# A hybrid attention and SSD layer: head-pair scores in three groups of six banks, and ScalarE emptying every product bank

## The chip, the cores and the metric

The kernel runs on one core of a Trainium2 chip. The time is the device time of one execution in microseconds, and what counts is the median of the runs. One execution was also profiled; the numbers of the trace come from that one.

## What is computed

One decoder layer on a sequence of 1024 tokens, 1024 wide, in float32. A modulated RMS norm feeds one input projection, whose columns are queries, keys, values and a gate of 16 attention heads (64 wide) and the inputs of a Mamba-2 SSD mixer with its own gate. Cut to what matters here:

```python
proj = h @ w_in                     # 1024 x 6672
# attention, per head, swept over 128-query blocks:
z = einsum("bqhd,bkhd->bhqk", q[:, start:end], k[:, :end]) * 64**-0.5
log_one_minus = where(mask, log_sigmoid(-z), 0.0)
tail = cumsum(log_one_minus, axis=3, reverse=True) - log_one_minus
weights = exp(where(mask, log_sigmoid(z) + tail, -inf))
o = einsum("bhqk,bkhd->bqhd", weights, v[:, :end])
y_attn = rms_norm(o, sb_norm_gain) * silu(z_attn)
# SSD: conv, softplus(dt), chunked scan in 128-token chunks
y_ssm = rms_norm(y * silu(z_ssm), ssm_norm_gain)
x = x + gate * (concat([y_attn, y_ssm]) @ w_out)
return rms_norm(x, norm_f_gain)
```

## The kernel before

Float32 products are made of three matmuls: an operand is split into a rounded high part and the rest (`whi`, `wlo`; `hh`, `hl`), and high times high, high times low and low times high are added up in one bank of PSUM. A product of 128 features by 1024 tokens (`inproj_f`) goes in two halves of 512 columns, each 24 matmuls into one bank of the pool `pj`.

The program has a first part (norm, modulation, convolution inputs), a middle one (the SSD scan), and from about 311 us on the attention of eight head pairs. From there the order of instructions on each engine is the order in which the code is written (`K` and `pinned`). The attention needs little of TensorE at a time and waits on ScalarE and VectorE, so it is laced into the remaining matrix products, called the side work (`inproj_f`, `inproj_v`, `outproj`): `ROUND` lists the steps of one pair, and after each of them `fill` runs side steps. `left` says how many microseconds of the current bank's product are still to come, `tick` advances a planned clock, and on it `late` emits ScalarE's and VectorE's share of the attention little by little.

The steps of a pair, both heads (`e` = 0, 1) together:
- `scores` ("s"): the products of queries and keys. Each head uses 64 rows of TensorE's array, so the two heads run side by side (mode 64 x 128). `GROUPS` says which query blocks `i` and which columns stand in which bank. A group takes four banks of the pool `pz`, and there are five groups per pair.
- `sigmoids` on ScalarE from each bank into `om` (or `bc`) and `be` (or `bs`), then `scan` and `weights` on VectorE, which leave the weights in `be` / `bs`.
- `turned` ("t"): 128 x 128 transposes of the weights on TensorE, two banks at a visit, copied back by ScalarE. One bank is of the pool `pt`, the second of `pj`, the pool of the side products.
- `values` ("v"): weights times values, each head in 64 columns of the array (mode 128 x 64), in the bank `pv`.

PSUM has eight banks: `pj` 2, `pz` 4, `pt` 1, `pv` 1. A side product's bank is emptied in different ways: queries and keys by ScalarE twice (`qk`); the two gates by a ScalarE function and then by a VectorE instruction that reads the bank again (`zgate_evac`, `gate_ssm`, L959 and L848); the SSD output projection by VectorE alone (`out_ssm`, L1227). `by_v` and `slow` mark such products. `turn` is the last gate's product, laced with loading and splitting `w_out`; `front` and `back` do that for the attention half.

Of the kernel before, what the change touches and what calls it, by code (L numbers as in the profile page):

```python
# [14 lines left out]
P = 128  # L15
# [11 lines left out]
def hybrid_layer_kernel(  # L27
# [68 lines left out]


# [88 lines left out]
    left, slow = [0.0], [False]  # L186
# [111 lines left out]
    def inproj_f(col, evac, between=None, by_v=False):  # L298


        wts = take(2) if pinned[0] else split_f(load_f(col))
        for b in range(2):
            ps = bank(pj, "pj")
            for k in range(KT):
                mm_f(ps, wts, k, b)
                if pinned[0]:
                    ahead()
                    if b and k % 4 == 3:
                        used()
                left[0], slow[0] = 0.7 * (KT - 1 - k), by_v  # L310
                yield 0.7
            evac(b, ps)
            if between:
                yield between(b)

    def inproj_v(vc, with_dt, v_tiles, dt_raw, extra=None):
# [19 lines left out]
        for i in range(TB):  # L336
            ps = bank(pj, "pj")
            ts_ = slice(i * P, (i + 1) * P)
            for k in range(KT):
# [500 lines left out]
    def gate_ssm(j):  # L840
        box = []

        def evac(b, ps):
            if b == 0:
                box.append(mk(sp, "th", [P, S], bufs=1))
            th, sl = box[0], slice(b * HALF, (b + 1) * HALF)
            A.activation(th[:, sl], ps, AF.Tanh, scale=0.5)
            V.scalar_tensor_tensor(th[:, sl], th[:, sl], 1.0, ps, op0=ALU.add, op1=ALU.mult)  # L848
            V.tensor_tensor(xs[j][:, sl], xs[j][:, sl], th[:, sl], op=ALU.mult)

        yield from inproj_f(C_ZS + j * P, evac, by_v=True)
# [77 lines left out]
    def qk(p, box):  # L929
# [3 lines left out]
        def evac(b, ps):  # L933
# [19 lines left out]
    def zgate_evac(p):  # L953
        def evac(b, ps):
# [4 lines left out]
            V.scalar_tensor_tensor(zg, zg, cols[:, 92 + p:93 + p], ps, op0=ALU.mult, op1=ALU.mult)  # L959
# [3 lines left out]
    def zgate(p):  # L963
        yield from inproj_f(C_Z + p * P, zgate_evac(p), by_v=True)
# [3 lines left out]
    GROUPS = {7: ((7, 0, 512, 0, 0), (7, 512, 512, 1, 0)), 6: ((6, 0, 512, 0, 0), (6, 512, 384, 1, 0)),  # L968
# [3 lines left out]


    ROUND = (("s", 7, 0), ("t", 3, -1), ("t", 2, -1), ("v", 2, -1), ("v", 0, -1), ("s", 6, 0), ("t", 7, 0),
             ("s", 5, 0), ("t", 6, 0), ("s", 4, 0), ("t", 5, 0), ("t", 1, 0), ("s", 3, 0), ("t", 4, 0),
             ("t", 0, 0), ("f", 0, 0), ("v", 6, 0), ("v", 4, 0))
# [9 lines left out]
    def scores(p, g):  # L986
        qh, ql, kh, kl = box[p]
        flush("A", lambda: not late["A"])
        n_ = seq["made"]
        flush("V", lambda: len(seq["scanned"]) >= n_ - 1)  # L990
        seq["made"] += 1
        if g % 2:
            tiles[p, g // 2] = [duo() if g > 3 else mk(sp, "bs", [P, 2, HALF], bufs=2) for _ in range(2)]
        oms = [mk(op, "om", [P, 1028], bufs=2), mk(sp, "bc", [P, S], bufs=4)]
        parts = []
        zs = [[bank(pz, "pz") for _ in range(2)] for _ in range(2)]
        for i, c0, cw_, b, z0 in GROUPS[g]:
            mw = max(cw_, 256)

            for n, (a, k_) in enumerate(((qh, kh), (qh, kl), (ql, kh))):  # L1000
                for e in range(2):
                    r = slice(64 * e, 64 * e + 64)
                    K(T.matmul(zs[b][e][:, z0:z0 + mw], a[r, i * P:(i + 1) * P], k_[r, c0:c0 + mw],  # L1003
                               start=(n == 0), stop=(n == 2)))
            parts.append((i, c0, cw_, [z[:, z0:z0 + cw_] for z in zs[b]]))
        off = {i: 0 if i == g else (g + 1) * P for i, _, _, _ in parts}

        def sigmoids(i, c0, cw_, z, e):
# [3 lines left out]
            be, om = tl[e][:, i % 2, x0:x0 + W], oms[e][:, off[i] + c0:off[i] + c0 + cw_]  # L1012
# [6 lines left out]
        def scan(i, e):  # L1019
            W = (i + 1) * P  # L1020
            om = oms[e][:, off[i]:off[i] + W]

            diag, rest = om[:, W - P:W][:, ::-1], om[:, 0:W - P][:, ::-1]
            V.tensor_tensor_scan(diag, diag, ident[:, ::-1], 0.0, op0=ALU.mult, op1=ALU.max)
            if i:
                V.tensor_tensor_scan(rest, rest, rest, om[:, W - P:W - P + 1],
                                     op0=ALU.mult, op1=ALU.bypass)

        def weights(i, e):
            W = (i + 1) * P  # L1030
            tl, x0 = place(p, i)
            be, om = tl[e][:, i % 2, x0:x0 + W], oms[e][:, off[i]:off[i] + W]
            V.memset(be[:, W - 1:W], 0.0)
            V.tensor_tensor(be[:, :W - 1], be[:, :W - 1], om[:, 1:W], op=ALU.mult)
            seq["weights"].add((p, i, e))
            if e == 1 and i == parts[-1][0]:
                seq["scanned"].append((p, g))

        for e in range(2):
            for i, c0, cw_, zs in parts:  # L1040
                cost = 0.3 + 1.6e-3 * cw_
                late["A"].append((cost, lambda i=i, c0=c0, cw_=cw_, z=zs[e], e=e: sigmoids(i, c0, cw_, z, e)))
        tick(1.8)

    def turned(p, i):

        banks = [(e, j0, min(i + 1, j0 + 4)) for e in range(2) for j0 in range(0, i + 1, 4)]

        while banks:
            wide = sum(b[2] - b[1] for b in banks[:2]) > 4  # L1050
            while wide and side_left() and left[0] >= 0.0 and not 1.3 < left[0] < (2.2 if slow[0] else 3.6):
                side_step()
            n = 1 if wide and left[0] < 0.0 else 2
            go, banks = banks[:n], banks[n:]
            for e, _, _ in go:
                if (p, i, e) not in seq["weights"]:
                    flush("A", lambda: (p, i, e) in seq["weights"] or not late["A"])
                    flush("V", lambda: (p, i, e) in seq["weights"])
            room, used_, copies = bank(pt, "pt"), 0, []
            for e, j0, j1 in go:  # L1060
                tl, x0 = place(p, i)
                be = tl[e][:, i % 2, x0:x0 + (i + 1) * P]
                if used_ + j1 - j0 > 4:
                    room, used_ = bank(pj, "pj"), 0
                for j in range(j0, j1):
                    K(T.transpose(room[:, (used_ + j - j0) * P:(used_ + j - j0 + 1) * P],  # L1066
                                  be[:, j * P:(j + 1) * P], ident))
                copies.append((be[:, j0 * P:j1 * P], room[:, used_ * P:(used_ + j1 - j0) * P]))
                used_ += j1 - j0
            for to, from_ in copies:  # L1070
                A.copy(to, from_)
            tick(0.11 * sum(j1 - j0 for _, j0, j1 in go))
            fill(sum(0.5 + 0.1 * (j1 - j0) for _, j0, j1 in go), True)

    def values(p, i0):
        (tl, x0), hb, q0 = place(p, i0), i0 // 4, i0 % 4
        if i0 in (6, 2):
            while side_left() and clock[0] < free_at[0]:
                side_step()
            pav[p] = bank(pv, "pv")  # L1080
        for j in range(i0 + 2):
            u = int(j > i0)
            for e in range(2):
                K(T.matmul(pav[p][64 * e:64 * e + 64, (q0 + u) * P:(q0 + 2) * P],  # L1084
                           vs[p][:, j * P + 64 * e:j * P + 64 * e + 64],
                           tl[e][:, u:2, x0 + j * P:x0 + (j + 1) * P], start=(j == 0), stop=(j > i0)))
        tick(0.2 * i0 + 0.4)
        if i0 in (6, 2):
            return
        sl = slice(hb * HALF, (hb + 1) * HALF)  # L1090
        if p == 0 and hb == 1:
# [12 lines left out]
        if hb == 0:
# [10 lines left out]
    def outproj(w_h, w_l, evac, first=None):  # L1115

        yt = take(2)
        for b in range(2):
            ps = first if first is not None and b == 0 else bank(pj, "pj")
            sl = slice(b * HALF, (b + 1) * HALF)  # L1120
            for k in range(KT):
# [7 lines left out]
                left[0], slow[0] = 0.7 * (KT - 1 - k), True  # L1129
# [11 lines left out]
    def turn():  # L1141
# [49 lines left out]
        for k, b in [(k, b) for k in range(6) for b in range(2)] + [(6, 0), (7, 0), (6, 1), (7, 1)]:  # L1191
# [21 lines left out]
    def out_ssm():  # L1213
# [6 lines left out]
        for i in range(TB):  # L1220
            t3 = []

            def evac(sl, ps):
                hooks["first"] = True
# [5 lines left out]
            yield from outproj(lambda k, b: wo_h[k][:, b * HALF:(b + 1) * HALF],  # L1230
                               lambda k, b: wo_l[k // 2, b][:, k % 2], evac, None if i else bank(pz, "pz"))
# [83 lines left out]
    def count(what, i):  # L1315
        if what == "s":
            return 4.0
        if what in "vf":
            return 0.0
        return 2 * sum(0.5 + 0.1 * (min(i + 1, j0 + 4) - j0) for j0 in range(0, i + 1, 4))  # L1320
# [47 lines left out]
    for p in range(9):  # L1368
        for what, i, before in ROUND:
# [142 lines left out]
```

## Time and profile before

| | |
|---|---|
| median of 3 runs | 1063.65 us (1063.28 to 1064.63) |
| the profiled execution: its time, its span | 1063.0 us, 1061.3 us |
| granted TensorE clock | 0.999 of full speed |
| TensorE matmul busy | 1039.0 us, 98% of the span |
| VectorE busy | 768.0 us, 72% |
| ScalarE busy | 528.6 us, 50% |
| the eight pairs, 311 to 925 us: TensorE, VectorE, ScalarE busy | 605.2, 456.0, 322.1 us of 614 |

A time is 1.7 us over the span in the profiled execution; the median is 0.65 us over that execution. A matmul's shown duration reaches past the start of the next one, because matmuls overlap in the array: what one costs is read from one start to the next.

### The profile page before, as it was taken

How to read it: one execution, taken by the hardware profiler on the slowest of the kernel's cores; microseconds unless marked ns; L12 is line 12 of the kernel's file. 1: busy time of each engine (PE TensorE's matmuls, PEld its weight loads, DVE VectorE, ACT ScalarE, POOL GpSimd, SP SyncE). 2: the span in 40 equal slices, each digit the busy share in tenths (PEclk: the TensorE clock that was granted, in tenths of full speed). 3: DMA queues.
4: the chain of work that ended last, by engine and by line, in shares of the span. 5: the costliest groups of instructions: out<-in, count | busy, mean ns of one | idle time of the engine just before them, and what ended most of it. 6: DMA issues, size and time to landing. Idle time of an engine off the chain costs nothing.

```text
span 1061.3 us, 16252 instructions
## 1 busy us (share of the span) xinstructions
PE 1039.0 (98%) x6317; PEld 844.2 (80%) x6317; DVE 768.0 (72%) x1339; ACT 528.6 (50%) x1162; POOL 2.6 (0%) x23
## 2 busy tenths in 40 slices
PE   7999999999999999999999999999999999999997
PEld 5789888777877787798787987878977777688886
DVE  5728779988848775656787758877668789665554
ACT  5755397676423553563554644646546646410111
POOL 0000000000000000000000000000000000000000
PEclk9999999999999999999999999999999999999999
DMA  9611332223202221101321103211111632665432
GB/s 350 229 41 31 92 112 79 74 95 129 71 20 70 80 70 31 60 21 41 91 59 61 31 21 90 76 35 41 39 52 30 199 97 74 204 210 174 155 110 79
DMA packets 91560, 96.15 MB, mean 91 GB/s; under 512 B 5998, under 2 KB 75994, under 8 KB 91484
## 3 DMA queue, kind: packets, MB, share of 16 engines
q1 hardware_dynamic: 88828, 86.45, 25.9%
q10 hardware_dynamic: 2656, 8.67, 2.4%
q8 instruction: 49, 0.80, 0.3%
q14 instruction: 27, 0.22, 0.1%
HBM read 78.26 MB, written 16.84 MB: 90 GB/s over the span
## 4 chain that ended last, share of the span: by engine, by line
PE 86%; DVE 8%; ACT 2%; issue 2%; DMA 1%; ACTq 0%; DVEq 0%; SPq 0%
PE pj L295 35%; PE pj L1125 13%; PE pv L1084 6%; PE pz L1003 5%; PE pz L553 3%; PE pt L1066 3%; PE pj L345 3%; PE pj L341 3%; PE pj L342 3%; DVE om L62 2%; PE pj L1066 2%; DVE bc L62 2%; PE pz L815 1%; PE pv L829 1%; PE pz L820 1%
## 5 line engine op out<-in xcount | busy, mean ns | idle before, releaser
L295 PE MATMUL pj<-hh,whi 128*128 128x512 f32 x544 | 222.2, 408 | 0.0
L295 PE MATMUL pj<-hh,wlo 128*128 128x512 f32 x544 | 214.1, 394 | 0.0
L295 PE MATMUL pj<-hl,whi 128*128 128x512 f32 x544 | 212.5, 391 | 0.0
L295 PEld LDWEIGHTS pj<-hh,whi 128*128 128x128 f32 x544 | 102.3, 188 | 24.5 <-issue 5.6
L295 PEld LDWEIGHTS pj<-hh,wlo 128*128 128x128 f32 x544 | 102.1, 188 | 22.7 <-issue 0.7
L295 PEld LDWEIGHTS pj<-hl,whi 128*128 128x128 f32 x544 | 102.5, 188 | 19.1 <-issue 1.0
L62 DVE TENSOR_TENSOR wlo<-raw,whi 128x512 fp32r<-128x512 f32 (+1 forms) x109 | 75.4, 692 | 23.1 <-ACT whi L62 16.7
L62 ACT COPY be<-pt 128x512 f32<-128x512 f32 (+2 forms) x98 | 47.1, 499 | 82.7 <-PE pt L1066 79.7
L62 ACT ACTIVATE be<-pz 128x255 f32<-128x255 f32 (+5 forms) x160 | 84.6, 531 | 0.0
L62 DVE TENSOR_TENSOR_SCAN om<-om 128x896 f32<-128x896 f32 (+6 forms) x56 | 71.9, 1285 | 2.0
L62 DVE TENSOR_TENSOR_SCAN bc<-bc 128x896 f32<-128x896 f32 (+6 forms) x56 | 71.9, 1285 | 2.0
L62 DVE TENSOR_TENSOR_SCAN om<-om,ident 128x128 f32<-128x128 f32 x64 | 26.9, 421 | 62.3 <-ACT om L62 62.2
L62 ACT ACTIVATE om<-pz 128x512 f32<-128x512 f32 (+1 forms) x96 | 48.0, 500 | 36.1 <-PE pz L1003 36.1
L341 PE MATMUL pj<-whi,hh 128*128 128x256 f32 (+1 forms) x224 | 65.1, 291 | 0.0
L1003 PE MATMUL pz<-big,big 64*128 64x512 f32 (+2 forms) x576 | 63.5, 354 | 1.1 <-ACT be L62 0.9
L345 PE MATMUL pj<-whi,hl 128*128 128x256 f32 (+1 forms) x224 | 64.4, 288 | 0.0
L342 PE MATMUL pj<-wlo,hh 128*128 128x256 f32 (+1 forms) x224 | 63.6, 284 | 0.0
L62 ACT ACTIVATE th<-v 128x1024 f32<-128x1024 f32 (+2 forms) x9 | 8.5, 943 | 103.7 <-DVE v L62 103.7
L1003 PEld LDWEIGHTS pz<-big,big 64*128 64x128 f32 x576 | 46.2, 184 | 17.3 <-issue 10.2
L62 DVE TENSOR_TENSOR be<-be,bc 128x1024 f32<-128x1024 f32 (+6 forms) x62 | 55.4, 894 | 1.3
L295 PE MATMUL pj<-hh,st 128*128 128x512 f32 x160 | 55.4, 399 | 0.0
L62 ACT ACTIVATE bc<-pz 128x512 f32<-128x512 f32 (+1 forms) x96 | 53.7, 559 | 0.0
(303 smaller groups left out, 2166.8 us busy)
## 6 DMA issues: line engine op xcount, KB each, us to landing
raw<-in_w_in_dram SPq DMA_DIRECT2D x98, 256.0 KB, 2.8
be<-acT_d ACTq DMA_DIRECT2D x16, 512.0 KB, 3.8
big<-in_x_dram SPq DMA_DIRECT2D x10, 512.0 KB, 6.9
aw<-in_w_ada_dram SPq DMA_DIRECT2D x16, 256.0 KB, 4.6
u_d<-big SPq DMA_DIRECT2D x8, 512.0 KB, 2.6
y_d<-bc SPq DMA_DIRECT2D x8, 512.0 KB, 3.0
raw<-in_w_ada_dram SPq DMA_DIRECT2D x16, 256.0 KB, 2.7
raw<-u_d SPq DMA_DIRECT2D x16, 256.0 KB, 2.9
```

The lines of the kernel that those rows point to most:

```text
L62: return lambda *args, **kw: K(op(*args, **kw))
L295: K(T.matmul(ps, w[:, ws], h[:, b * HALF:(b + 1) * HALF], start=(k == 0 and n == 0), stop=(k == KT - 1 and n == 2)))
L341: K(T.matmul(ps[:, :n], h_hi[k][:, ts_], whi[:, ws], start=(k == 0), stop=False))
L342: K(T.matmul(ps[:, :n], h_hi[k][:, ts_], wlo[:, ws], start=False, stop=False))
L345: K(T.matmul(ps[:, :n], h_lo[k][:, ts_], whi[:, ws], start=False, stop=(k == KT - 1)))
L553: K(T.matmul(acc[f][:, c0:c1], w[:, f * P:(f + 1) * P], h[:, sl], start=(k == 0 and n == 0 and c0 == 0), stop=(k == KT - 1 and n == 2)))
L815: K(T.matmul(po, xd[:, 0, h, :], m[:, h, :], start=True, stop=(ch == 0)))
L820: K(T.matmul(po, st[:, h, :], abc[:, h, :], start=False, stop=True))
L1003: K(T.matmul(zs[b][e][:, z0:z0 + mw], a[r, i * P:(i + 1) * P], k_[r, c0:c0 + mw], start=(n == 0), stop=(n == 2)))
L1066: K(T.transpose(room[:, (used_ + j - j0) * P:(used_ + j - j0 + 1) * P], be[:, j * P:(j + 1) * P], ident))
L1084: K(T.matmul(pav[p][64 * e:64 * e + 64, (q0 + u) * P:(q0 + 2) * P], vs[p][:, j * P + 64 * e:j * P + 64 * e + 64], tl[e][:, u:2, x0 + j * P ...
L1125: K(T.matmul(ps, y[:, ks], w(k, b), start=(k == 0 and n == 0), stop=(k == KT - 1 and n == 2)))
```

## The change

- Scores: three groups per pair ("s" 1, 2, 3), each in six banks: one of `pj`, the one of `pt`, four of `pz`. `STAND` says where a block stands in the two tiles per head. A 128-wide piece is computed 256 wide, as before, and one more such piece arises.
- `scores` runs side steps until the current side product has between 0.6 and 3.6 us left, and it lets all weights of the earlier groups be emitted first (before: of all but the last group).
- Transposes: `TURNS` lists the banks; the second bank of a visit is of `pz`, not `pj`. Block 0 goes with block 4, block 1 with block 2.
- Values: blocks 6, 7 and 2, 3 in one run, 4, 5 and 0, 1 in the other; the result of a run is two runs of columns of the bank.
- ScalarE empties all product banks while the pairs run: after its function it copies the bank to a tile `hf`, and VectorE reads the copy. In `out_ssm` that copy also scales.
- `by_v`, `slow` and the hook "first" go; in `turn` the order of the last steps changes and VectorE's splits are put 1.2 us later; `back` is called at the same values steps under their new names; a DMA scratch buffer is half as large.

```diff
+    def emptied(ps, scale=None):
+        full = mk(sp, "hf", [P, HALF], bufs=2)
+        if scale is None:
+            A.copy(full, ps)
+        else:
+            A.activation(full, ps, AF.Copy, scale=scale)
+        return full
...
 def gate_ssm(j):
-            V.scalar_tensor_tensor(th[:, sl], th[:, sl], 1.0, ps, op0=ALU.add, op1=ALU.mult)
+            full = emptied(ps) if pinned[0] else ps
+            V.scalar_tensor_tensor(th[:, sl], th[:, sl], 1.0, full, op0=ALU.add, op1=ALU.mult)
...
 def qk(p, box):
-                full = mk(sp, "th", [P, S], bufs=1)[:, sl]
-                A.copy(full, ps)
-                V.tensor_tensor(lo[:, sl], full, hi[:, sl].bitcast(F32), op=ALU.subtract)
+                V.tensor_tensor(lo[:, sl], emptied(ps), hi[:, sl].bitcast(F32), op=ALU.subtract)
...
 def zgate_evac(p):
-            V.scalar_tensor_tensor(zg, zg, cols[:, 92 + p:93 + p], ps, op0=ALU.mult, op1=ALU.mult)
+            V.scalar_tensor_tensor(zg, zg, cols[:, 92 + p:93 + p], emptied(ps), op0=ALU.mult, op1=ALU.mult)
...
-    GROUPS = {7: ((7, 0, 512, 0, 0), (7, 512, 512, 1, 0)), 6: ((6, 0, 512, 0, 0), (6, 512, 384, 1, 0)),
...
-    ROUND = (("s", 7, 0), ("t", 3, -1), ("t", 2, -1), ("v", 2, -1), ("v", 0, -1), ("s", 6, 0), ("t", 7, 0),
...
+    GROUPS = {1: ((7, 0, 512, 0, 0), (7, 512, 512, 1, 0), (3, 0, 512, 2, 0)),
+              2: ((6, 0, 512, 0, 0), (6, 512, 256, 1, 0), (1, 0, 256, 1, 256), (6, 768, 128, 2, 384), (2, 0, 384, 2, 0)),
+              3: ((5, 0, 512, 0, 0), (5, 512, 256, 1, 0), (4, 0, 256, 1, 256), (0, 0, 128, 2, 0), (4, 256, 384, 2, 128))}
+    STAND = {7: (0, 0), 3: (1, 0), 6: (0, 0), 1: (1, 384), 2: (1, 0), 5: (0, 0), 4: (1, 0), 0: (0, 768)}
+    ROUND = (("v", 6, -1), ("s", 1, 0), ("t", 5, -1), ("v", 4, -1), ("s", 2, 0), ("t", 7, 0), ("t", 3, 0),
+             ("s", 3, 0), ("t", 6, 0), ("t", 2, 0), ("f", 0, 0))
...
 def scores(p, g):
+        while side_left() and not 0.6 < left[0] < 3.6:
+            side_step()
-        flush("V", lambda: len(seq["scanned"]) >= n_ - 1)
+        flush("V", lambda: len(seq["scanned"]) >= n_)
-        oms = [mk(op, "om", [P, 1028], bufs=2), mk(sp, "bc", [P, S], bufs=4)]
+        oms = [[mk(op, "om", [P, 1028], bufs=2), mk(sp, "bc", [P, S], bufs=4)] for _ in range(2)]
+        zs = {(0, 0): bank(pj, "pj"), (1, 0): bank(pt, "pt")}
+        for at_ in ((2, 0), (0, 1), (1, 1), (2, 1)):
+            zs[at_] = bank(pz, "pz")
...
 def turned(p, i):
-                    room, used_ = bank(pj, "pj"), 0
+                room, at_ = bank(pz if n else pt, "pz" if n else "pt"), 0
...
 def values(p, i_):
+        ps = bank(pv, "pv")
+        for i0 in (i_, i_ - 4):
...
 def out_ssm():
-                V.scalar_tensor_tensor(t3[0][:, sl], ps, rstds["s"][:, i:i + 1], row["sum"][:, sl],
-                                       op0=ALU.mult, op1=ALU.mult)
+                full = emptied(ps, rstds["s"][:, i:i + 1])
+                V.tensor_tensor(t3[0][:, sl], full, row["sum"][:, sl], op=ALU.mult)
...
-    nc = _bacc.Bacc("TRN2", target_bir_lowering=False, num_devices=1, dynamic_dma_scratch_size=8192)
+    nc = _bacc.Bacc("TRN2", target_bir_lowering=False, num_devices=1, dynamic_dma_scratch_size=4096)
```

Where the instructions now stand. In the rows, a name's number tells one buffer's use from another's; L295 and L304 are the side product before and now, L1066 and L1093 the transposes, L1084 and L1120 the values, L1003 and L1028 the scores.

TensorE, the first visit to the transposes of block 7 in the fifth pair, before:

```order
L295 MATMUL pj_6364<-hh_396,wlo_892_6226 128x512
L1066 MATMUL pt_6392<-ident,be_6190 128x128 x4
L1066 MATMUL pj_6397<-ident,be_6190 128x128 x4
L295 MATMUL pj_6364<-hh_460,whi_897_6264 128x512
L295 MATMUL pj_6364<-hl_461,whi_897_6264 128x512
```

and now:

```order
L304 MATMUL pj_6533<-hh_460,wlo_907_6316 128x512
L1093 MATMUL pt_6563<-ident,be_6204 128x128 x4
L1093 MATMUL pz_6568<-ident,be_6204 128x128 x4
L304 MATMUL pj_6533<-hh_466,whi_906_6315 128x512
L304 MATMUL pj_6533<-hl_467,whi_906_6315 128x512
```

The second four transposes no longer ask for the `pj` bank that the side product before the current one has left, but for a `pz` bank.

TensorE, end of a values run and start of the next scores group, same pair, before:

```order
L1084 MATMUL pv_6312<-be_5678,v_4338 64x128
L1084 MATMUL pv_6312<-be_5679,v_4338 64x128
L1003 MATMUL pz_6331<-big_5647,big_5487 128x512
L1003 MATMUL pz_6332<-big_5647,big_5487 128x512
L1003 MATMUL pz_6331<-big_5648,big_5487 128x512
```

and now:

```order
L1120 MATMUL pv_6412<-be_5656,v_4343 64x128
L1120 MATMUL pv_6412<-be_5657,v_4343 64x128
L304 MATMUL pj_6403<-hh_390,whi_899_6272 128x512
L304 MATMUL pj_6403<-hl_391,whi_899_6272 128x512
L304 MATMUL pj_6403<-hh_390,wlo_900_6273 128x512
L1028 MATMUL pj_6442<-big_5738,big_5534 128x512
L1028 MATMUL pz_6445<-big_5738,big_5534 128x512
L1028 MATMUL pj_6442<-big_5739,big_5534 128x512
```

A scores group begins in `pj` and `pz`, and in seven of fourteen places side matmuls (three in five places, six and 24 in the others) now stand between values and scores.

ScalarE, emptying the second half of a gate's product (`bc<-pj`) in the same pair, before, where it stands among the sigmoids of a group:

```order
L62 ACTIVATE bc_6330<-pz_6332 128x512
L62 ACTIVATE be_6191<-pz_6332 128x512
L62 ACTIVATE bc_6254<-pj_6257 128x512
L62 ACTIVATE bc_6330<-pz_6334 128x384
L62 ACTIVATE be_6191<-pz_6334 128x383
```

and now, behind the copies of a transposes' visit:

```order
L62 COPY be_5657<-pz_6382 128x256
L62 COPY be_5657<-pz_6382 128x2x128
L62 ACTIVATE bc_6306<-pj_6311 128x512
L62 COPY hf_6400<-pj_6311 128x512
L62 ACTIVATE th_6429<-pv_6412 128x512
```

The copy to `hf` is new, and with it the bank is done with; VectorE's instruction that read the bank (L959, L967 now) stands as it did in VectorE's order, but reads `hf`.

More of the change, by code (lines that the diff above doesn't have):

```diff
@@ L1037, in weights @@
                 seq["scanned"].append((p, g))
         for e in range(2):
-            for i, c0, cw_, zs in parts:
+            for i, c0, cw_, z in parts:
                 cost = 0.3 + 1.6e-3 * cw_
-                late["A"].append((cost, lambda i=i, c0=c0, cw_=cw_, z=zs[e], e=e: sigmoids(i, c0, cw_, z, e)))
-        tick(1.8)
+                late["A"].append((cost, lambda i=i, c0=c0, cw_=cw_, z=z[e], e=e: sigmoids(i, c0, cw_, z, e)))
+        tick(2.4)
     def turned(p, i):
-        banks = [(e, j0, min(i + 1, j0 + 4)) for e in range(2) for j0 in range(0, i + 1, 4)]
+        banks = list(TURNS[i])
@@ L1049, in turned @@
         while banks:
[L1050 to L1063, printed above, removed]
-                    room, used_ = bank(pj, "pj"), 0
[L1065 to L1069, printed above, removed]
+            go, banks = banks[:2], banks[2:]
@@ new lines, in turned @@
+            need = {(p, b, e) for parts in go for e, b, _, _ in parts}
+            if not need <= seq["weights"]:
+                flush("A", lambda: need <= seq["weights"] or not late["A"])
+                flush("V", lambda: need <= seq["weights"])
+            copies, width = [], 0
+            for n, parts in enumerate(go):
+                room, at_ = bank(pz if n else pt, "pz" if n else "pt"), 0
+                for e, b, j0, j1 in parts:
+                    tl, x0 = place(p, b)
+                    be = tl[e][:, b % 2, x0:x0 + (b + 1) * P]
+                    from_ = room[:, at_ * P:(at_ + j1 - j0) * P]
+                    for j in range(j0, j1):
+                        K(T.transpose(from_[:, (j - j0) * P:(j - j0 + 1) * P], be[:, j * P:(j + 1) * P], ident))
+                    at_ += j1 - j0
+                    if b == 0:
+                        to = tl[e][:, 0, 4 * P:8 * P].rearrange("p (u t) -> p u t", u=2)[:, :, 0:P]
+                        copies[-1] = (to, room[:, (at_ - 2) * P:at_ * P].rearrange("p (u t) -> p u t", u=2))
+                    else:
+                        copies.append((be[:, j0 * P:j1 * P], from_))
+                width += at_
@@ L1070, in turned @@
             for to, from_ in copies:
                 A.copy(to, from_)
[L1072 to L1091, printed above, removed]
+            tick(0.11 * width)
@@ new lines, in turned, with turn_cost, values @@
+            fill(turn_cost(go), True)
+    def turn_cost(banks):
+        return sum(0.5 + 0.1 * (j1 - j0) for bank_ in banks for _, _, j0, j1 in bank_[:1])
+    def values(p, i_):
+        while side_left() and clock[0] < free_at[0]:
+            side_step()
+        ps = bank(pv, "pv")
+        for i0 in (i_, i_ - 4):
+            (tl, x0), q0 = place(p, i0), i0 // 4 * 2
+            for j in range(i0 + 2):
+                u = int(j > i0)
+                for e in range(2):
+                    K(T.matmul(ps[64 * e:64 * e + 64, (q0 + u) * P:(q0 + 2) * P],
+                               vs[p][:, j * P + 64 * e:j * P + 64 * e + 64],
+                               tl[e][:, u:2, x0 + j * P:x0 + (j + 1) * P], start=(j == 0), stop=(j > i0)))
+            tick(0.2 * i0 + 0.4)
+        if p == 0 and i_ == 6:
@@ L1113, in gate_row, with outproj @@
         return 1.1
-    def outproj(w_h, w_l, evac, first=None):
+    def outproj(w_h, w_l, evac):
         yt = take(2)
         for b in range(2):
-            ps = first if first is not None and b == 0 else bank(pj, "pj")
+            ps = bank(pj, "pj")
             sl = slice(b * HALF, (b + 1) * HALF)
@@ L1316, in count @@
         if what == "s":
-            return 4.0
+            return 6.0
         if what in "vf":
             return 0.0
-        return 2 * sum(0.5 + 0.1 * (min(i + 1, j0 + 4) - j0) for j0 in range(0, i + 1, 4))
+        return turn_cost(TURNS[i])
     PER_PAIR = sum(count(what, i) for what, i, _ in ROUND)
@@ L1380, in hybrid_layer_kernel @@
                     side_step()
-                while (p, i) == (7, 7) and "first" not in hooks:
-                    side_step()
                 scores(p, i)
-                fill(4.0 if i != 3 else 2.0)
+                fill(6.0)
             if (p, what, i) == (6, "f", 0):
```

87 lines of the change are left out of this document (50 added, 37 removed), and 3 rows, old and new, of the table GROUPS.

## Prediction

> **What bounds the kernel now.** I read the page first, then the stretch of the head pairs, then who waits for whom on TensorE, and then single rows of TensorE's timeline.
>
> ```profile
> span 1061.3 us, 16252 instructions
> PE 1039.0 (98%) x6317; PEld 844.2 (80%) x6317; DVE 768.0 (72%) x1339; ACT 528.6 (50%) x1162; POOL 2.6 (0%) x23
> PE 86%; DVE 8%; ACT 2%; issue 2%; DMA 1%; ACTq 0%; DVEq 0%; SPq 0%
> ```
>
> TensorE is busy 98% of the span and carries 86% of the chain that ended last. The time of the kernel is therefore the sum of what TensorE's instructions cost plus the few microseconds in which it stands. The change touches only the stretch of the eight pairs (311 to 925 us); up to there the order of all five engines is the same in both kernels, and behind it the same side matmuls are left (584 and 593, the difference having been used earlier).
>
> ```profile
> core 0: us, PE busy (x) PEld busy (x) DVE busy (x) ACT busy (x) POOL busy (x), PEclk, DMA share, GB/s
> 311.00:925.00 614.00, 605.20 (x3844) 489.80 (x3841) 456.01 (x794) 322.10 (x764) 0.00 (x0) 1.00 0.22 66
> ```
>
> Here TensorE stands 614.0 - 605.2 = 8.8 us. ScalarE and VectorE have 292 and 158 us to spare, so on average neither is a bound. Whom TensorE stands for, in the same stretch (waited for, us in total, times, longest):
>
> ```profile
> PE pj L1066 <- DVE bc L62: 3.0, 4, 1.0
> PE pj L1066 <- DVE v L62: 1.4, 1, 1.4
> PE pj L1066 <- DVE th L62: 1.3, 2, 0.9
> PE pj L1066 <- DVE be L62: 1.1, 1, 1.1
> PE pz L1003 <- ACT be L62: 0.9, 1, 0.9
> PE pt L1066 <- ACT be L62: 0.5, 1, 0.5
> PE pj L1125 <- ACT be L62: 0.3, 1, 0.3
> PE pz L1003 <- DVE big L62: 0.2, 1, 0.2
> ```
>
> The first four rows are 6.8 us in 8 waits, all of transposes that write a `pj` bank (the second bank of a visit). What they wait for is seen in one of them, in TensorE's timeline and VectorE's (start, duration, idle before in brackets):
>
> ```profile
> 653.72 0.60 PE L1066 MATMUL pt<-ident,be 128*128 128x128 f32 x4
> 655.30 0.66 PE L1066 MATMUL pj<-ident,be 128*128 128x128 f32 x4 [0.98 <-DVE bc L62]
> 654.51 0.74 DVE L62 SCALAR_TENSOR_TENSOR bc<-bc,cols,pj 128x512 f32<-128x512 f32 x1
> ```
>
> The four transposes into `pj` start at 655.30, when VectorE ends (654.51 + 0.74 = 655.25) the instruction that reads the gate's `pj` bank. So it is not the weights that are late but a bank: VectorE has scans and splits in its queue ahead of the reading.
>
> **What a change of the array's mode costs.** Transposes first, then scores:
>
> ```profile
> 600.27 0.28 PE L345 MATMUL pj<-whi,hl 128*128 128x256 f32 x1
> 600.39 0.60 PE L1066 MATMUL pt<-ident,be 128*128 128x128 f32 x4
> 600.82 0.49 PE L1066 MATMUL pj<-ident,be 128*128 128x128 f32 x3
> 601.07 0.36 PE L341 MATMUL pj<-whi,hh 128*128 128x256 f32 x1
> 601.27 0.28 PE L342 MATMUL pj<-wlo,hh 128*128 128x256 f32 x1
> ...
> 590.28 0.40 PE L295 MATMUL pj<-hl,st 128*128 128x512 f32 x1
> 590.51 0.40 PE L295 MATMUL pj<-hh,st 128*128 128x512 f32 x1
> 590.84 1.67 PE L1003 MATMUL pz<-big,big 64*128 64x512 f32 x18
> 592.43 0.50 PE L295 MATMUL pj<-hh,whi 128*128 128x512 f32 x1
> 592.77 0.39 PE L295 MATMUL pj<-hl,whi 128*128 128x512 f32 x1
> ```
>
> Seven transposes and one 256-wide matmul (0.12 us, 600.27 to 600.39) take 601.27 - 600.39 = 0.88 us, 0.109 us a transpose: entering and leaving transposes costs nothing. Scores are different. A 512-wide side matmul goes every 0.23 us (590.28 to 590.51); the last one ahead of the scores takes 0.33 and the first one behind them 0.34, 0.21 us more together. Inside, three groups give the price of a pair of score matmuls (the two heads side by side):
>
> ```profile
> 602.68 1.50 PE L1003 MATMUL pz<-big,big 64*128 64x384 f32 x18
> 604.11 0.39 PE L341 MATMUL pj<-whi,hh 128*128 128x256 f32 x1
> 616.10 1.49 PE L1003 MATMUL pz<-big,big 64*128 64x512 f32 x12
> 617.52 0.39 PE L341 MATMUL pj<-whi,hh 128*128 128x256 f32 x1
> ```
>
> The group of 512, 256 and 256 columns takes 1.59 us (590.84 to 592.43), that of 384, 256 and 256 takes 1.43, that of 512 and 384 takes 1.42, each three times over. With 0.19 us of entering and leaving inside each (what fits the rate of the side matmuls, 0.44 ns a column) a pair costs 0.233, 0.176 and 0.118 us at 512, 384 and 256 columns. So a scores group between side matmuls pays 0.21 + 0.19 = 0.40 us for two changes of mode, 0.20 us each.
>
> The Trainium skill, TensorEngine Tiling (Array Packing), Key Properties, says that changing the tiling mode drains TensorE; its page TensorE: Matmul & The Clock Gate, Single matmul latency, puts a drain at about 0.175 us. By that, as an estimate, the next term would be 4.6 us, not 5.2. I keep the rows.
>
> **The change part by part.**
>
> *Changes of mode.* In TensorE's order I count 99 of them before (40 scores runs, 16 values runs, 13 times values directly ahead of scores) and 73 now (24, 16, 7 times). 26 x 0.20 = -5.2 us. Six of the boundaries move from values ahead of scores to values ahead of side work, whose prices no row above shows apart; I take both at 0.20. Were the first free, the term would be -4.0, were the second free, -6.4.
>
> *Wider scores.* Per pair, in threes: 384-wide pieces go from 3 to 2, 256-wide from 4 to 6, 512-wide stay 5. (2 x 0.118 - 0.176) x 3 x 8 = +1.4 us. Transposes (576) and values (320) stay the same in number. 98 visits to transposes become 80, at nothing.
>
> *The second bank of a visit.* It moves from `pj` to `pz`, which ScalarE alone empties. The 8 waits go: 6.8 us of idleness, and each was longer by what the modelled duration hides (653.72 to 655.30 is 1.58 us against 0.43 from 600.39 to 600.82: 1.15 lost, 0.98 shown), 8 x 0.16. In all -8.1 us. The 0.9 us of scores waiting for a `pz` bank stands where the first bank of `out_ssm` had been taken from `pz`, which goes too, and the 0.3 us at L1125 is a wait for a transposes' copy out of `pj`: -1.2 us.
>
> *ScalarE's copies.* From the groups by shape:
>
> ```profile
> L62 ACT CAST big<-pj 128x512 fp32r<-128x512 f32 x32 | 20.2, 631 | 44.2 <-PE pj L295 44.1
> L62 ACT COPY th<-pj 128x512 f32<-128x512 f32 x28 | 18.2, 652 | 0.0
> L62 ACT ACTIVATE om<-pz 128x512 f32<-128x512 f32 x40 | 24.0, 599 | 27.4 <-PE pz L1003 27.4
> L62 ACT ACTIVATE om<-pz 128x256 f32<-128x256 f32 x24 | 9.6, 402 | 0.0
> L62 ACT ACTIVATE big<-big,cols 128x512 f32<-128x512 f32 x8 | 5.3, 722 | 0.0
> ```
>
> New are 16 copies for the gates of the attention and 8 for the SSD gates (0.652 us each, 15.6 us), 16 scaled ones in `out_ssm` (0.722, 11.6 us), and 4 more sigmoids a pair, 32, at the fixed part of one (0.402 - 256 x 0.197/256 = 0.205 us, 6.6 us): 34 us on ScalarE, where 292 us are free. VectorE keeps its instructions. On average this is nothing; what it may cost is in bursts. The sigmoids of a group are now up to 20 in a row, some 8 us by these rows (before, 8 to 12), and behind them in ScalarE's queue stand the emptying of the next side bank and the copies of the transposes. TensorE needs the other `pj` bank only when the current half product ends, up to 3.6 us later by `left`, and the bank that the scores took is the first that the sigmoids free. Half a product lasts 24 x 0.23 = 5.5 us, emptying it 0.63 + 0.65 us. Bounds: 0 if the pacing holds, 24 groups x 1.28 us = 31 us if every group waits for one whole emptying. The nearest rows are TensorE's waits for ScalarE above, 0.9 + 0.5 + 0.3 = 1.7 us in the whole stretch; I take +2.0.
>
> *Two `om` buffers used by one group, `bc` two at a time.* The sigmoids of a group now wait until VectorE has left the group before, and behind them waits the emptying. VectorE has 456 of 614 us to do. What it has for a group has grown: between the first scores of the fifth pair and the transposes of its block 7 stand 57 side matmuls before and 99 now, 13 and 23 us. 0, inside the +2.0. That `scores` emits all earlier weights first moves work forward in VectorE's queue, at no cost to TensorE while side weights are split two pieces ahead.
>
> *The rest.* `out_ssm`: VectorE reads a tile instead of a bank, same count. `turn`: splits 1.2 us later; they are needed by `out_ssm` after 40 side matmuls (9 us), 0. The stores of the results of a pair and the loads of `back` keep their places behind the values; the last store is needed 168 side matmuls (39 us) later, 0. The smaller DMA scratch: the page lists hardware queues and instruction loads only, 0.
>
> Sum: -5.2 + 1.4 - 8.1 - 1.2 + 2.0 = -11.1 us. The profiled execution took 1063.0 us, so 1051.9; the median stands 0.65 above it, so 1052.6 us, said as 1053.
>
> **The rivals.**
>
> *Fewer waits go than I think (1060 us).* Only the modes and widths come in, -3.8, and TensorE stands for ScalarE or for late weights as long as it stood for VectorE's banks. For it: the 8 waits end with VectorE, and VectorE's queue is as long as before. Against it: the row at 654.51 shows what was read, and that bank is ScalarE's now. 1063.65 - 3.8 = 1060.
>
> *ScalarE's burst holds the banks (slower, about 1082 us).* Each of 24 groups makes TensorE wait for one emptying of `pj`, 31 us, against the 11.1 + 2.0 = 13.1 us won: 1063.65 + 31 - 13 = 1082. It decides from 13.1 / 24 = 0.55 us a group. For it: one engine now empties everything, and 34 us are added to it. Against it: 292 us free, and the place in the half product at which scores may start leaves at least 5.5 - 3.6 = 1.9 us for an emptying of 1.28. The Trainium skill, TensorEngine Tiling (Array Packing), PSUM Bottleneck, says that tiling speeds up TensorE but not the emptying of PSUM and advises ScalarE and VectorE for it together; that rule speaks for this rival. By the row of the 8 waits, sharing with VectorE is what cost the time here.
>
> *The gain is real but taken back (no change, 1063 us).* `scores` waits for its place in the side product and for six banks at once; if TensorE stands 0.5 us at each group for `pt` or `pz`, 12 us are gone. Against it: a transposes' copy takes half a microsecond, and 9 side matmuls (2 us) or more lie between the last visit and a group.
>
> **How the numbers follow.** My forecast 0.62 (1050 to 1057), fewer waits go 0.20 (1057 to 1061), taken back 0.07 (1061 to 1066), the burst 0.11 (above 1066, up to 1082). A measurement here tells about 0.2%, 2.1 us, from no change. So faster 0.83, same 0.06, slower 0.11. The range: below, all 8.8 us of idleness and its hidden part go and nothing is added, -5.2 + 1.4 - 10.1 = -13.9, 1049.7; above, the first rival, 1060.5 with its own spread. Outside lie the last two and a tail, 0.2.
>
> **What would show it.** Scores visits fall to 24 and cost, from the side matmul ahead to the second behind, 0.40 us more than their pairs. No row of TensorE's waits has transposes waiting for `pj`. TensorE's idleness between the first scores and the last values is 2 to 3 us instead of 8.8. ScalarE is busy about 560 us on the page. I am wrong if new rows of scores or side matmuls waiting for ScalarE add up to more than 4 us, if the price of a change of mode depends on what stands on its two sides, or if transposes now wait for weights.

## The result and the profile after

The changed kernel takes 1049.1 us (median of 4 runs, 1048.9 to 1049.6), the kernel before 1063.5 us beside it (4 runs, 1062.9 to 1064.6): a ratio of 0.9864 (95% interval 0.9847 to 0.9881), 14.4 us less. Forecast were 1053 us, and by the prediction's sums a range of 1049.7 to 1060.5. The sign was right and the waits that were named did go, but the time lies 0.6 us below the range.

The page of the kernel after, first its span, its engines and the chain that ended last, and below that the stretch of the eight pairs (columns as in the row of before):

```profile
span 1047.1 us, 16416 instructions
PE 1031.9 (99%) x6365; PEld 847.2 (81%) x6365; DVE 766.5 (73%) x1339; ACT 547.8 (52%) x1218; POOL 2.7 (0%) x23
PE 93%; DVE 2%; ACT 2%; DMA 2%; issue 0%; SPq 0%; DVEq 0%; ACTq 0%
```

```profile
313.00:913.00 600.00, 598.30 (x3893) 493.09 (x3894) 456.77 (x798) 337.09 (x815) 0.00 (x0) 1.00 0.23 69
```

TensorE now carries 93% of the chain instead of 86%; what VectorE had of it (8%) is 2%. In the stretch TensorE stands 600.0 - 598.3 = 1.7 us instead of 8.8, and its busy time falls from 605.2 to 598.3. So of some 14 us half is shown as idleness that went, and half as busy time. That busy half isn't all cheaper work, as will be seen: a matmul's shown duration can hide a wait.

Whom TensorE waits for, in the kernel after, over the whole span:

```profile
PE pv L125 <- DMA cbm<-in_norm_in_gain_dram: 5.4, 1, 5.4
PE pj L1163 <- ACT hf L62: 1.1, 1, 1.1
PE pj L350 <- ACT v L62: 0.5, 1, 0.5
```

The first lies outside the pairs, as do three rows of 0.4 us and less that are left out. Of all waits of transposes for `pj` none is left. New are two waits for ScalarE, 1.6 us together. The larger one, in TensorE's rows and ScalarE's:

```profile
826.45 0.39 PE L1232 MATMUL pj<-hh,wlo 128*128 128x512 f32 x1
825.71 1.22 ACT L62 CAST woh<-wor 128x512 fp32r<-128x512 f32 x2 [0.19 <-DMA wor<-in_w_out_dram]
826.84 0.59 ACT L62 ACTIVATE bc<-pj 128x512 f32<-128x512 f32 x1
827.33 0.58 ACT L62 COPY hf<-pj 128x512 f32<-128x512 f32 x1
827.96 0.50 PE L1163 MATMUL pj<-woh,st 128*128 128x512 f32 x1 [1.12 <-ACT hf L62]
```

This isn't a burst of sigmoids. ScalarE rounds two pieces of `w_out` that had come late from a DMA, then empties the gate's bank (0.59 + 0.58 us), and TensorE's next half starts when `hf<-pj` ends at 827.91. The smaller one stands behind a burst, in ScalarE's rows and TensorE's:

```profile
465.19 0.49 ACT L62 COPY v<-pj 128x128 f32<-128x128 f32 x2
465.73 0.38 PE L350 MATMUL pj<-whi,hh 128*128 128x256 f32 x1 [0.48 <-ACT v L62]
```

From 462.95 us to the copy of the bank that TensorE needs, ScalarE works through six sigmoids.

A visit of eight transposes, like the one shown before (653.72 and 655.30), and a scores group between side matmuls:

```profile
655.67 0.60 PE L1093 MATMUL pt<-ident,be 128*128 128x128 f32 x4
656.11 0.60 PE L1093 MATMUL pz<-ident,be 128*128 128x128 f32 x4
```

```profile
509.02 0.40 PE L304 MATMUL pj<-hh,wlo 128*128 128x512 f32 x1
509.35 0.50 PE L1028 MATMUL pj<-big,big 64*128 64x512 f32 x1
...
510.75 1.16 PE L1028 MATMUL pz<-big,big 64*128 64x256 f32 x13
511.84 0.50 PE L304 MATMUL pj<-hh,whi 128*128 128x512 f32 x1
512.17 0.40 PE L304 MATMUL pj<-hl,whi 128*128 128x512 f32 x1
```

The second four transposes start 0.44 us behind the first four, where it was 1.58. The group costs from 509.02 to 512.17 3.15 us: two side matmuls (0.46), the pairs at the prediction's prices (3 x (0.233 + 3 x 0.118 + 0.176) = 2.29), and 0.40 for two changes of mode, as forecast.

### The profile page after: what moved, and what is told of

Its sections match the earlier page's. It is cut to its first block, busy times and chain, and to the rows that moved or that the text cites. A ratio compares the mean times of both kernels' runs of the same rounds, so it can differ in the third digit from the quotient of the medians.

```text
span 1047.1 us, 16416 instructions
## 1 busy us (share of the span) xinstructions
PE 1031.9 (99%) x6365; PEld 847.2 (81%) x6365; DVE 766.5 (73%) x1339; ACT 547.8 (52%) x1218; POOL 2.7 (0%) x23
## 4 chain that ended last, share of the span: by engine, by line
PE 93%; DVE 2%; ACT 2%; DMA 2%; issue 0%; SPq 0%; DVEq 0%; ACTq 0%
PE pj L304 40%; PE pj L1163 16%; PE pv L1120 6%; PE pt L1093 3%; PE pz L562 3%; PE pj L350 3%; PE pj L354 3%; PE pj L351 3%; PE pz L1093 3%; PE pj L1028 2%; PE pz L1028 2%; PE pt L1028 2%; PE pz L824 1%; PE pv L838 1%; PE pz L829 1%; PE pj L1497 1%
## 5 line engine op out<-in xcount | busy, mean ns | idle before, releaser
L304 PE MATMUL pj<-hh,whi 128*128 128x512 f32 x544 | 220.2, 405 | 0.0
L304 PE MATMUL pj<-hh,wlo 128*128 128x512 f32 x544 | 214.0, 393 | 0.0
L304 PE MATMUL pj<-hl,whi 128*128 128x512 f32 x544 | 212.5, 391 | 0.0
L304 PEld LDWEIGHTS pj<-hh,whi 128*128 128x128 f32 x544 | 102.2, 188 | 23.9 <-issue 5.5
L304 PEld LDWEIGHTS pj<-hh,wlo 128*128 128x128 f32 x544 | 102.1, 188 | 22.6 <-issue 0.7
L304 PEld LDWEIGHTS pj<-hl,whi 128*128 128x128 f32 x544 | 102.4, 188 | 19.9 <-issue 1.0
L62 DVE TENSOR_TENSOR_SCAN om<-om 128x896 f32<-128x896 f32 (+2 forms) x48 | 87.3, 1818 | 1.7
L62 ACT COPY be<-pt 128x512 f32<-128x512 f32 (+1 forms) x80 | 38.6, 503 | 64.6 <-PE pt L1093 63.9
L1028 PE MATMUL pz<-big,big 64*128 64x256 f32 (+2 forms) x432 | 59.7, 334 | 0.0
L62 DVE TENSOR_TENSOR be<-be,om 128x767 f32<-128x767 f32 (+2 forms) x64 | 56.9, 889 | 3.1 <-DVE be L62 0.4
L62 ACT ACTIVATE be<-pz 128x127 f32<-128x127 f32 (+4 forms) x112 | 58.6, 529 | 0.0
L62 DVE TENSOR_TENSOR_SCAN bc<-bc 128x128 f32<-128x128 f32 (+2 forms) x64 | 56.6, 885 | 2.2
L304 PE MATMUL pj<-hh,st 128*128 128x512 f32 x160 | 56.1, 400 | 0.0
L1120 PE MATMUL pv<-be,v 128*64 128x256 f32 (+1 forms) x512 | 53.7, 362 | 0.0
L62 ACT ACTIVATE be<-be,acum 128x128 f32<-128x128 f32 x128 | 39.5, 390 | 24.5 <-DMA be<-acT_d 19.3
L1120 PEld LDWEIGHTS pv<-be,v 128*64 128x64 f32 x512 | 34.8, 137 | 20.1 <-issue 4.7
L62 DVE CAST whi<-raw 128x512 fp32r<-128x512 f32 x75 | 31.3, 418 | 23.2 <-PE pj L354 16.0
```

The costliest lines, as they stand in the source:

```text
L62: return lambda *args, **kw: K(op(*args, **kw))
L304: K(T.matmul(ps, w[:, ws], h[:, b * HALF:(b + 1) * HALF], start=(k == 0 and n == 0), stop=(k == KT - 1 and n == 2)))
L1028: K(T.matmul(zs[b, e][:, y0:y0 + mw], a[r, i * P:(i + 1) * P], k_[r, m0:m0 + mw], start=(n == 0), stop=(n == 2)))
L1120: K(T.matmul(ps[64 * e:64 * e + 64, (q0 + u) * P:(q0 + 2) * P], vs[p][:, j * P + 64 * e:j * P + 64 * e + 64], tl[e][:, u:2, x0 + j * P:x0 ...
```

## The experiments

The rivals after the result: (A) the waits for VectorE's banks were larger than their rows show; (B) the regrouping, that is mode changes and their price, was worth more than forecast; (C) something else in the change paid. The first four kernels were timed beside a kernel before of 1063.82 us (7 runs), the other four beside one of 1063.83 us.

| kernel | median, us | ratio to before, 95% |
|---|---|---|
| e1_old_pz | 1053.62 | 0.9905 (0.9890 to 0.9920) |
| e2_old_act | 1052.66 | 0.9898 (0.9883 to 0.9912) |
| e3_old_act_pz | 1052.28 | 0.9891 (0.9874 to 0.9907) |
| e4_new_dve | 1055.03 | 0.9913 (0.9895 to 0.9931) |
| e5_after_again | 1049.25 | 0.9861 (0.9845 to 0.9876) |
| e6_split_values | 1054.07 | 0.9905 (0.9889 to 0.9921) |
| e7_join_values_scores | 1048.05 | 0.9853 (0.9831 to 0.9875) |
| e8_narrow | 1049.08 | 0.9860 (0.9845 to 0.9875) |

### Another bank for the transposes, nothing else

```diff
 # turned, kernel before
-                    room, used_ = bank(pj, "pj"), 0
+                    room, used_ = bank(pz, "pz"), 0
```

> The kernel before with one edit: the second bank of a transposes' visit is taken from pz instead of pj; VectorE goes on reading product banks, scores stay in five groups. If a wait costs what it adds from one start to the next on TensorE (8.9 us for all waits inside a visit in the trace of before, 8.1 of them in the 8 long ones), it gains 8 to 9 us: 1055. If a wait costs only the idleness that the waits show (6.8 us): 1056.7. If the waits were not for the bank but for VectorE's weights: within 2 us of 1063.5.

Measured: 1053.62 us, 10.2 us less than before, where 8 to 9 were expected. One word of the change gives about 70% of its gain. TensorE's waits in the pairs, in this kernel:

```profile
PE pz L1003 <- ACT be L62: 0.9, 1, 0.9
PE pt L1066 <- ACT be L62: 0.6, 1, 0.6
PE pz L1003 <- DVE big L62: 0.2, 1, 0.2
```

All four rows of transposes waiting for VectorE are gone; the scores' wait at L1003 still stands. Added up from one start to the next, the 98 visits to the transposes take 55.2 us here and 64.0 before: 8.8 us, in the same order of instructions. That is what the prediction's 6.8 us of idleness, or 8.1 with its hidden part, cost. The whole stretch of the pairs is 9.9 us shorter by its starts. Nearly all of the rest, 0.9 us, lies at two places in L1125, where side matmuls waited for a `pj` bank that transposes had taken; those waits went with the same word.

### ScalarE empties the banks, in the old order and grouping

```diff
 # kernel before, with emptied() of the kernel after; shown for one of four places
-            V.scalar_tensor_tensor(zg, zg, cols[:, 92 + p:93 + p], ps, op0=ALU.mult, op1=ALU.mult)
+            V.scalar_tensor_tensor(zg, zg, cols[:, 92 + p:93 + p], emptied(ps), op0=ALU.mult, op1=ALU.mult)
```

> The kernel before with one edit: ScalarE copies every product bank of the pairs' stretch to a tile and VectorE reads the copy; transposes' second bank stays in pj, scores in five groups. If the waits are for VectorE's turn at the bank, ScalarE frees it about 1.2 us after the product's end and most of the 8 waits go too: 1056 to 1058. If ScalarE as the only emptier is late (the rival of the prediction): 1063 or more.

The edit also has the change's smaller DMA scratch buffer, and queries and keys go through `hf` instead of `th`; neither was run alone. Measured: 1052.66 us, 11.2 us less, more than the 1056 to 1058 that were expected. Transposes still write `pj`, but the bank is now free in time. Its waits in the pairs:

```profile
PE pt L1074 <- ACT be L62: 1.5, 1, 1.5
PE pj L1133 <- ACT be L62: 0.3, 1, 0.3
PE pz L1011 <- DVE big L62: 0.2, 1, 0.2
```

The longest wait is again at the late `w_out` (first what holds ScalarE up, then its copy `be<-pt`, for which the transposes wait):

```profile
826.36 0.62 ACT L62 CAST woh<-wor 128x512 fp32r<-128x512 f32 x1 [1.54 <-DMA wor<-in_w_out_dram]
826.88 0.26 ACT L62 COPY be<-pt 128x128 f32<-128x128 f32 x1
827.20 0.44 PE L1074 MATMUL pt<-ident,be 128*128 128x128 f32 x2 [1.54 <-ACT be L62]
```

This isn't shown to be a price of the copies: TensorE waits at the same place for the same reason in the kernel before (0.5 us at 833.50) and in the one with another bank alone (0.6 us at 825.45), both without the copies. No row shows a wait behind a burst of sigmoids. The scores' wait of 0.9 us at L1003 is gone here and still stood with the other bank alone. ScalarE's copy leaves the `pz` bank of the SSD output projection early (`hf<-pz` at 844.13), where VectorE read it only at 845.55 in that kernel: so this wait too seems to have come from a bank that VectorE kept, though its row names ScalarE.

### Both, in the old grouping

> Both edits in the kernel before, without the new groups, runs and order. If they are two remedies for the same waits, the gain is that of the first alone or up to 1 us more: 1054 to 1055.5. If they add up: 1049 or less, and the new grouping would be worth nothing.

Its edits are those of the two kernels above. Measured: 1052.28 us, 11.5 us less (1054 to 1055.5 were expected), 0.4 us less than with the copies alone. The two are remedies for the same waits and don't add up: alone they gave 10.2 and 11.2. So the waits were worth about 11 us (10.2 to 11.5), and (A) holds. What the grouping adds on top is 1052.28 - 1049.25 = 3.0 us by the medians, against the prediction's 3.8 (5.2 - 1.4); by the starts of the profiled executions, of which the first lay 1.7 us above its median, the pairs' stretch shrinks by 4.3 us (603.9 to 599.6). The two values lie on both sides of 3.8, so (B) isn't the main cause; a part of it of some 0.5 us can be neither shown nor excluded. For (C) nothing of that size is left over, but its parts (the order in `turn`, the runs of values, the DMA scratch buffer) were not run alone.

### The new grouping without ScalarE's copies

```diff
 # gate_ssm, zgate_evac, out_ssm of the kernel after; shown for one of the three
-            V.scalar_tensor_tensor(zg, zg, cols[:, 92 + p:93 + p], emptied(ps), op0=ALU.mult, op1=ALU.mult)
+            V.scalar_tensor_tensor(zg, zg, cols[:, 92 + p:93 + p], ps, op0=ALU.mult, op1=ALU.mult)
```

> The changed kernel with VectorE reading the banks of the two gates and of the SSD output projection again (no copies by ScalarE there); groups, runs and pz transposes stay. If the copies are needed because the scores' first bank is now the one of pj that VectorE would still hold, TensorE waits at scores: 2 to 8 us over the changed kernel, 1051 to 1057. If pz for the transposes was the whole remedy: within 1 us of 1049.

Measured: 1055.03 us (1052.5 to 1055.7), 5.8 us above the kernel after: in the new order the copies are needed. Of its four runs, the one with the highest granted clock (0.999) took 1052.5 us, 3.2 above; the three others (0.996 to 0.997) took 1054.7 to 1055.7. Its three longest waits in the pairs, and the place of the longest:

```profile
PE pj L1162 <- DVE bc L62: 3.5, 1, 3.5
PE pj L304 <- DVE bc L62: 0.8, 1, 0.8
PE pj L1027 <- DVE be L62: 0.7, 1, 0.7
```

```profile
828.13 0.59 ACT L62 ACTIVATE bc<-pj 128x512 f32<-128x512 f32 x1
828.62 0.69 DVE L62 TENSOR_TENSOR wol<-wor,woh 128x512 fp32r<-128x512 f32 x1
829.23 0.82 DVE L62 TENSOR_TENSOR be<-be,bc 128x639 f32<-128x639 f32 x1
829.96 0.68 DVE L62 TENSOR_TENSOR wol<-wor,woh 128x512 fp32r<-128x512 f32 x1
830.57 0.74 DVE L62 SCALAR_TENSOR_TENSOR bc<-bc,cols,pj 128x512 f32<-128x512 f32 x1
831.36 0.50 PE L1162 MATMUL pj<-woh,st 128*128 128x512 f32 x1 [3.51 <-DVE bc L62]
```

ScalarE is done with the bank at 828.72. VectorE reads it from 830.57 to 831.31, behind two splits of `w_out` and an attention product, and TensorE starts at 831.36: 2.6 us for the second reader of a bank, after a queue of other work (in the kernel after, ScalarE's second reading follows its first). The waits shown are 3.9 us more than the 1.1 of the kernel after at this place (3.5 + 0.8 + 0.7 - 1.1); 1.6 us more come from the clock, in the last section. One scores group waits as well (L1027, until 882.89), as its first bank is of `pj`, which VectorE reads until 882.84. Beside the prediction's passage from the Trainium skill (TensorEngine Tiling (Array Packing), PSUM Bottleneck: ScalarE and VectorE together): in the two orders tried here, ScalarE emptying alone was the faster arrangement, by 11.2 us in the old order and 5.8 in the new (3.2 by the run with the clock at 0.999).

### The kernel after once more

> The changed kernel as it is, as the point of comparison for the three others on the same chip: 1049 us.

Measured: 1049.25 us (1048.9 to 1049.4), 0.15 us from the first measurement. It is the yardstick for the next three.

### More changes of mode

```diff
 # values, kernel after
         for i0 in (i_, i_ - 4):
+            if i0 < 4 and side_left():
+                side_step()
```

> The changed kernel with a side step between the two blocks of each values run (where side work is left): 100 changes of the array's mode instead of 73, the same matmuls. If a change costs 0.20 us, 27 of them add 5.4 us (4.8 if entering values costs 0.15 as in the trace of before): 1054. If the gain that the prediction missed is in the changes, at 0.31 us each, 8.4 us: 1057.5.

Measured: 1054.07 us, 4.8 us above the control, for 100 changes of mode instead of 73: 4.8 / 27 = 0.18 us each (0.15 to 0.21 by the ends of the runs, 1053.3 to 1054.5 against 1048.9 to 1049.4). By the starts of the two profiled executions the stretch of the pairs is 5.4 us longer, of which 0.4 is a longer wait for ScalarE (1.4 us instead of 1.0). A split run in TensorE's timeline:

```profile
551.70 3.46 PE L1122 MATMUL pv<-be,v 128*64 128x256 f32 x32
555.10 0.50 PE L304 MATMUL pj<-hh,whi 128*128 128x512 f32 x1
555.43 0.40 PE L304 MATMUL pj<-hl,whi 128*128 128x512 f32 x1
555.67 0.39 PE L304 MATMUL pj<-hh,wlo 128*128 128x512 f32 x1
555.99 1.74 PE L1122 MATMUL pv<-bs,v 128*64 128x256 f32 x16
```

The three side matmuls between the two parts take from 555.10 to 555.99 0.89 us, where 3 x 0.23 = 0.69 is their price without a change: 0.20 more outside the values, the rest inside, as with scores. The prediction's 0.20 us a change holds for values too.

### Fewer changes of mode

```diff
 # values, kernel after
-        while side_left() and clock[0] < free_at[0]:
+        while side_left() and (clock[0] < free_at[0] or not 0.6 < left[0] < 3.6):
             side_step()
```

> The changed kernel with the side steps that place a scores group taken ahead of the values run, not between values and scores: 67 changes of mode instead of 73. At 0.20 us a change it gains 1.2 us, at 0.31 us 1.9 us. If the values then wait for copies or TensorE for a bank: no gain.

Measured: 1048.05 us (1047.0 to 1050.0), 1.2 us below the control for 6 changes fewer, 0.20 each. By the starts of the two profiled executions the stretch is 1.0 us shorter. The ranges of the runs overlap, so this is a sign and no proof, though only by the slowest run, the one with the lowest granted clock (0.996); the other three (1047.0 to 1048.2) lie below all runs of the control. It is the fastest kernel of the study.

### Narrow pieces computed narrow

```diff
 # scores, kernel after
-            m0, mw, y0 = (c0, cw_, z0) if cw_ > P else (max(c0 - P, 0), 256, z0 - P if c0 else z0)
+            m0, mw, y0 = c0, cw_, z0
```

> The changed kernel with the 128-wide pieces of the scores computed 128 wide instead of 256 (48 pairs of score matmuls). If a score matmul costs by its columns (a pair 0.118 us at 256), a pair at 128 costs about 0.06 and it gains 2.8 us: 1046. If TensorE takes a pair of 128 columns at the rate of the transposes (0.109 us for 128 columns), the gain is 0.4 us or less; if its rate falls further below 256 columns, it is slower.

Measured: 1049.08 us, 0.2 us below the control, within what can be told. The group that stands above at 509.35 to 511.84 (2.49 us) takes here 2.46:

```profile
509.41 0.50 PE L1028 MATMUL pj<-big,big 64*128 64x512 f32 x1
...
511.87 0.50 PE L304 MATMUL pj<-hh,whi 128*128 128x512 f32 x1
```

Three of its pairs are 128 wide instead of 256, so a pair of half the width is 0.01 us cheaper: a pair of 128 columns still costs about 0.11 us, against 0.118 at 256, and the columns computed twice are nearly free. Narrower pairs were not run.

## Why the prediction was right or wrong, point by point

**The step that failed: the size of the waits that go.** The terms of -8.1 us (transposes) and -1.2 us (scores, L1125) gave 9.3. Added up over the stretch from one start to the next, against what the same matmuls cost undisturbed, TensorE lost 12.5 us before and loses 2.4 now. The eight long waits were sized rightly: 8.1 us lost. Missed were those that show little idleness or none. The prediction gave the hidden part, 0.16 us, to eight waits only; the others it took at their shown idleness or, where nothing was shown, at nothing. Three such places in the kernel before, in TensorE's timeline:

```profile
850.34 1.19 PE L1003 MATMUL pz<-big,big 64*128 64x512 f32 x7
852.47 0.97 PE L1003 MATMUL pz<-big,big 64*128 64x512 f32 x5 [0.94 <-ACT be L62]
853.37 0.50 PE L1125 MATMUL pj<-woh,st 128*128 128x512 f32 x1
...
894.25 0.40 PE L1125 MATMUL pj<-woh,st 128*128 128x512 f32 x1
894.68 0.50 PE L1125 MATMUL pj<-woh,whi 128*128 128x512 f32 x1
...
902.72 0.40 PE L1125 MATMUL pj<-woh,wlo 128*128 128x512 f32 x1
903.39 0.50 PE L1125 MATMUL pj<-woh,whi 128*128 128x512 f32 x1 [0.28 <-ACT be L62]
```

The first group of rows is the last scores group: it takes 853.37 - 850.34 = 3.03 us, where the same twelve matmuls take 1.58 to 1.60 in six other pairs. It shows 0.94 of idleness and loses 1.4. The row at 894.68 shows no idleness at all, and still 894.68 - 894.25 = 0.43 us pass where 0.23 is the rate: 0.20 lost. The row at 903.39 shows 0.28 and loses 0.67 - 0.23 = 0.44. These last two gaps are gone in the kernel with another bank alone, so they were waits. Of some 3.2 us that were missed (12.5 less 9.3), 1.1 were at scores (this group and the first one), 0.9 waits ahead of transposes (shown as 0.5 us for `pt`, not priced at all), 0.7 inside transposes' visits, for the most part 0.06 us on the start behind each long wait, and 0.6 at side matmuls. The Trainium skill, Perfetto Trace Analysis, Tensor Engine Instruction, says why this is to be expected: the end of a matmul in a trace is an estimate from its size. The row at 894.25 agrees: it shows 0.40 us, where 0.23 is the rate.

**The range fell with it.** Its lower end was built on the claim that 10.1 us is all that waits can give. The waits gave just that as a balance (12.5 gone, 2.4 new), and modes and widths came out above their term, so the time came out 0.6 us under the end. With the waits read from starts, the sum is -5.2 + 1.4 - 12.5 + 2.0 = -14.3, or 1049.4 us, 0.3 above what was measured.

**Changes of mode and wider scores, -5.2 + 1.4.** Right in the main. 0.40 us a group stands in the rows after, 0.18 to 0.20 a change came from two experiments. The stretch is 14.5 us shorter by its starts, the waits are 10.1 of it, which leaves 4.4 for this term of 3.8. Where the 0.6 lies isn't settled; 0.02 us on each of 26 changes would be enough, and by the medians (3.0 us) the term came out below 3.8. The drain of 0.175 us that the Trainium skill gives (TensorE: Matmul & The Clock Gate, Single matmul latency), weighed in the prediction, is nearly as near to the measured 0.18 to 0.20; the runs can't tell the two apart.

**The order of the values' boundaries.** Taken at one price for both, with -4.0 and -6.4 as ends. The rows bear out one price. In the kernel after, the last step of the values takes 0.20 us instead of 0.10 ahead of scores and of side matmuls alike; behind it the first pair of scores takes 0.34 instead of 0.23, and so does the first side matmul. That is about 0.2 us for either boundary.

**The second bank of a visit.** Right as a mechanism: one word of code takes the waits away. Not foreseen was that ScalarE's copies alone do the same, and that the two are therefore one gain; the prediction put the gain on the bank alone, and counted ScalarE's copies at nothing but their risk.

**New waits for ScalarE, +2.0.** Measured 1.6 shown, 2.1 lost, and 0.3 at a visit to the transposes that shows no idleness. The size was right and the mechanism half: one comes behind a burst (0.5 us), the larger one from ScalarE waiting for `w_out`. At that place, 825 to 833 us, the kernel after and every variant that was run has its longest wait of the pairs, the one with another bank alone its second longest.

**ScalarE's work.** Forecast about 560 us on the page, measured 547.8. The 40 copies alone made it 549.7 (from 528.6), 0.53 us each instead of 0.65 and 0.72; rows of neighbours overlap on ScalarE (above, `bc<-pj` runs until 827.43 and `hf<-pj` starts at 827.33).

**The rivals.** *Fewer waits go* (1060): refuted, no row shows transposes waiting. *Taken back*: refuted, no row of scores waits for a bank. *The burst holds the banks* (from 0.55 us a group): two waits, one of them behind a burst, 2.1 us lost in 24 groups, 0.09 us a group.

## What to carry to other kernels

Size a wait on TensorE from the starts of the matmuls around it, not from the idleness shown, and look for gaps that show none: here 12.5 us were lost where 8.8 were shown. A PSUM bank that a second engine reads again is free only when that engine's queue gets there; give the bank to a tile by the engine that read it first, or give the next user another bank, and expect the gain of only one of the two. Group the work of one array mode, at 0.2 us a change, and leave transposes where they are.

## What the runs showed of the hardware that was not expected

TensorE's long wait in the new order without the copies (3.5 us) had an aftermath. The granted clock (the third figure from the end) in windows behind it, of that kernel:

```profile
831.40:832.40 1.00, 1.00 (x3) 0.86 (x4) 1.00 (x2) 1.00 (x3) 0.00 (x0) 0.67 1.06 387
832.40:833.20 0.80, 0.80 (x3) 0.61 (x3) 0.80 (x3) 0.80 (x2) 0.00 (x0) 0.50 1.04 396
834.80:836.00 1.20, 1.20 (x6) 0.97 (x5) 1.20 (x3) 1.20 (x4) 0.00 (x0) 0.85 0.38 108
```

For 3.4 us, from 831.74, the clock is at half, and a 512-wide matmul goes every 0.43 us instead of 0.23: the nine that start from 831.70 on take 3.64 us instead of 2.07, 1.6 us on top of the wait. The shorter waits (1.1 us in the kernel after, 1.5 in the one with the copies alone) had no such row. The Trainium skill, TensorE: Matmul & The Clock Gate, Part 1: The HAM clock gate, gives an idle window of about 3.4 us for the fall to half clock. The wait of 3.5 us agrees, but the ends of the ten traces don't bear 3.4 us out as a limit: behind the shown end of TensorE's last matmul the clock falls after 2.5 us (the kernel with fewer changes of mode: matmul until 1039.15, half clock from 1041.68) to 5.0 us (the kernel after). So a wait of 2.5 us can be enough; between 1.5 and 2.5 us no trace shows anything.

Second, a pair of score matmuls costs about 0.11 us at 128 columns and 0.118 at 256: half the columns saved 0.01 us.
